# 204 low parts of weights from GpSimd to VectorE, with wider rotary tables and later gate rows

## The chip, the cores and the metric

The kernel runs on one core of a Trainium2 chip. The metric is the device time of one execution in microseconds. Three runs of the kernel before the change took 2226.13, 2218.59 and 2211.78 us; their median is 2218.59 us.

The engines are named as the profile names them: PE is the matrix engine (TensorE), DVE is VectorE, ACT is ScalarE, POOL is GpSimd, SP is SyncE, which here only issues DMA transfers.

## The reference

The kernel computes two layers of a hybrid decoder trunk on x of 1024 rows by 1024 columns, all in float32. The core of a layer:

```python
ada = c_act @ w_ada[l] + b_ada[l]
shift, scale, gate = jnp.split(ada, 3, axis=-1)
h = rmsnorm(x, norm_g[l]) * (1.0 + scale[:, None, :]) + shift[:, None, :]
p = h @ w_in[l]
mq, mk, mv, mo, mz, mi, mf, rq, rk, rv, rz = split_cols(p)
...
y_m = jax.nn.sigmoid(mo) * head_layernorm(cell, gn_m[l], N_HEADS_MLSTM) * jax.nn.silu(mz)
rq_h = rotary(rq.reshape(B, S, N_HEADS_RET, HD_R), positions)
rk_h = rotary(rk.reshape(B, S, N_HEADS_RET, HD_R), positions)
ret = retention_chunkwise(rq_h, rk_h, rv.reshape(B, S, N_HEADS_RET, HD_R))
y_r = head_layernorm(ret, gn_r[l], N_HEADS_RET) * jax.nn.silu(rz)
y = jnp.concatenate([y_m, y_r], axis=-1) @ w_out[l]
x = x + gate[:, None, :] * y
```

`rotary` multiplies halves of q and k by the cosine and the sine of position times a frequency per column. Four heads (0 to 3) are an mLSTM with a short causal convolution on q and k, four (4 to 7) are a retention. Each works in chunks and carries a state from chunk to chunk. A root mean square norm ends the trunk.

## The kernel before

Every matrix product is made of three: a float32 operand is split into a high part, which is the operand cast to the type that PE multiplies fast (float32r), and a low part, which is the operand minus its high part. `mm3` then multiplies high by high (L181), high by low (L182) and low by high (L183). For weights, `high` is a cast on ACT (L408, tile `wH`) and `low` is a subtraction of two 128 by 512 tiles (L413, tile `R`); its last argument names the engine, POOL unless said otherwise.

The work of a layer has three stages. In the **product stage** the columns of `w_in` are taken in jobs: a `plan` string gives their order (v for values of two heads, z, q, k and a for gates, queries, keys and output gates). A job multiplies a two by two block of weights by the hidden state with seven products instead of eight (named a11, a12, a22, S1 to S4), whose weights are sums of the blocks. A weight tile is loaded into `R`; for S1 and S3 a second block is added by a DMA that POOL issues (L714), for S2 and S4 the sum is made on DVE (L718). `Feeder.quad` states when, counted in slots (one slot is one product), a tile is loaded, cast and subtracted: the low part two slots ahead of its product. Products gather in four PSUM banks, two named px and two named pz, which DVE and ACT empty (L780 to L840). In front of the first job `build_forms` makes the sums of the hidden state (L639 to L660), whose high and low parts `split_to` makes on ACT and POOL (L881, L882).

**Attention** runs beside the later jobs of the product stage, one head after the other, by a table of steps. Its splits of q and k are L881 on ACT and L882 on POOL, that of the scores L1083 and L1084 (`sL`), that of the state L1107 and L1109 (`cL`); L934 makes the low part of the keys, L1185 a power on POOL that the norm's L1188 needs. For mLSTM heads the convolution is L894 on DVE. The **output projection** follows; its low parts are made on DVE for the first half of the columns and on POOL for the second.

Two side jobs run as generators beside the products; `yield n` lets n slots pass. `rotary_tables` (layer 0) makes the turns whose sines are taken later; all its DVE calls go through the wrapper in `Later`, so that the profile shows them at L148. `gate_rows` (layer 1, started by `adaptive`) loads sixteen rows of 256 KB through `ada_rows`, multiplies and sums them on DVE (L312, L314), adds a bias, splits the sum, spreads it over all partitions with PE (L350) and stores it. The output projection of layer 1 reads it back.

The order on PE is the order of the code. The orders on DVE, ACT, POOL and SP come from a scheduler that places instructions when the program is built; each engine then works through its list strictly in order. `late` keeps an instruction in the code's order.

Of the kernel before, what the change touches and what calls it, by code (L numbers as in the profile page):

```python
# [13 lines left out]
I32 = mybir.dt.int32  # L14
AF = mybir.ActivationFunctionType
ALU = mybir.AluOpType
# [3 lines left out]
P = 128  # L20

D = 1024
T = 1024
# [4 lines left out]
HALF = 512  # L28
CH = 256
# [8 lines left out]
NACC = 12  # L38
# [49 lines left out]
def tile_hybrid_trunk(ctx, tc, x, xt, c, positions, w_ada, b_ada, norm_g, w_in, w_blk, w_val, conv_w, conv_b,  # L88
                      b_igate, b_fgate, gn_m, gn_r, w_out, final_g, consts, out):
    nc = tc.nc  # L90
    V, A, G, PE, Q = nc.vector, nc.scalar, nc.gpsimd, nc.tensor, nc.sync
# [37 lines left out]
    turn = [0]  # L129
# [23 lines left out]
    def launch(gen, delay=0, last=0):  # L153
        uid[0] += 1
        pending.append([clock[0] + delay, uid[0] + last * 1000000, gen])
# [160 lines left out]
    def ada_columns_later(l):  # L316
        cl = cols[l][0]
        for half in range(2):
            k = 4 * half
            for which in range(2):  # L320
                accs = []
                yield from ada_rows(l, which * D + half * 512, accs)
                yield 1
                pt = ps_a()
                for i in range(4):
                    PE.matmul(pt[:, i:i + 1], accs[0][:, i * P:(i + 1) * P], ones, start=True, stop=True)
                yield 1
                if which:
                    t1 = wt("sm1", 4, 2)
                    V.scalar_tensor_tensor(t1, pt[:, 0:4], 1.0, cl[:, 112 + k:116 + k], ALU.add, ALU.add)  # L330
                    V.tensor_tensor(gsh[l][:, 0, k:k + 4], t1, cl[:, k:k + 4], ALU.mult)
                else:
                    V.tensor_tensor(gsh[l][:, 1, k:k + 4], pt[:, 0:4], cl[:, 104 + k:108 + k], ALU.add)

    def gate_rows(l):
        for half in range(2):
            accs = []
            yield from ada_rows(l, 2 * D + half * 512, accs)
            brow = wt("acc", 512, NACC)
            Q.dma_start(brow[0:1, :], b_ada[l, 2 * D + half * 512:2 * D + (half + 1) * 512].unsqueeze(0))  # L340
            yield 1
            acc = accs[0]
            V.tensor_tensor(acc[0:1, :], acc[0:1, :], brow[0:1, :], ALU.add)
            yield 1
            a2 = (wt("wH", 512, NW, F32R), wt("R", 512, NR, F32R))
            split_to(a2, acc)
            yield 2
            pt = ps_a()
            for i in range(2):
                PE.matmul(pt, ones_r, a2[i], start=i == 0, stop=i == 1)  # L350
            yield 1
            g = wt("acc", 512, NACC)
            V.tensor_copy(g, pt)
            yield 1
            Q.dma_start(gbd[half], g)

    def adaptive(l, gcol, gb):
        if l + 1 < DEPTH:
            yield from ada_columns_later(l + 1)
            yield from gate_cols(l, gcol)  # L360
        else:
            yield from gate_rows(l)

    def gate_cols(l, gcol):
        for half in range(2):
            accs = []
            yield from ada_rows(l, 2 * D + half * 512, accs)
            yield 2
            pt = ps_a()
            for i in range(4):  # L370
                PE.matmul(pt[:, i:i + 1], accs[0][:, i * P:(i + 1) * P], ones, start=True, stop=True)
            V.tensor_tensor(gcol[:, 4 * half:4 * half + 4], pt[:, 0:4],
                            cols[l][0][:, 120 + 4 * half:124 + 4 * half], ALU.add)
            yield 1
# [23 lines left out]
    def w_block(l, c0, p):  # L398
        return w_blk[l, (c0 - 8 * (c0 > OFF_I)) // P, p]
# [41 lines left out]

    rdr = [[dpool.tile([P, HALF], F32, name=f"rdr{i}{j}") for i in range(2)] for j in range(2)]

    def rotary_tables():
        V = Later()
        c1, c2, c3 = two_pi_split()
        ts = [wt("acc", 512, NACC) for _ in range(3)]
        ang, turn, tmp, rnd, a1, pos = (t[:, i * CH:(i + 1) * CH] for t in ts for i in range(2))
        a2 = ang
        for n in range(4):  # L450
            i, cs = n // 2, slice((n % 2) * CH, (n % 2 + 1) * CH)
            if n == 0:
                Q.dma_start(pos.bitcast(I32), positions[0:1, 0:CH].to_broadcast([P, CH]))
                yield 2
            V.tensor_copy(ang, pos.bitcast(I32))
            if n < 3:
                Q.dma_start(pos.bitcast(I32), positions[0:1, (n + 1) * CH:(n + 2) * CH].to_broadcast([P, CH]))
            V.tensor_scalar(ang, ang, kc[:, C_FREQ:C_FREQ + 1], None, ALU.mult)
            V.tensor_copy(a1.bitcast(F32R), ang)
            V.tensor_tensor(a2, ang, a1, ALU.subtract)  # L460
            V.tensor_scalar(turn, a1, c3, None, ALU.mult)
            V.scalar_tensor_tensor(turn, a2, c3, turn, ALU.mult, ALU.add)
            V.scalar_tensor_tensor(turn, a2, c2, turn, ALU.mult, ALU.add)
            yield 1
            for src, cc in ((a1, c2), (a2, c1), (a1, c1)):
                V.tensor_scalar(tmp, src, cc, None, ALU.mult)
                V.tensor_scalar(rnd, tmp, MAG_I, -MAG_I, ALU.add, ALU.add)
                V.tensor_tensor(tmp, tmp, rnd, ALU.subtract)
                V.tensor_tensor(turn, turn, tmp, ALU.add)
                yield 1  # L470
            parts = ((1, 0.0, tmp), (0, 0.25, a1))
            for which, sh, dst in parts:
                if sh:
                    V.tensor_scalar(turn, turn, sh, None, ALU.add)
                V.tensor_scalar(rnd, turn, MAG_I, -MAG_I, ALU.add, ALU.add)
                V.tensor_tensor(dst, turn, rnd, ALU.subtract)
                yield 1
                V.tensor_scalar(dst, dst, 0.49999994, -0.49999994, ALU.min, ALU.max)
            for which, sh, dst in parts:
                Q.dma_start(rdr[which][i][:, cs], dst)  # L480
            yield 1

    def gate_raw(l):
# [143 lines left out]
    def zcol(hg, m):  # L627
        return (OFF_MZ if hg < 4 else OFF_RZ) + (hg % 4) * HD + m * P

    def ocol(hg, m):  # L630
        return OFF_MO + hg * HD + m * P
# [29 lines left out]
            keep("U4", u4)  # L661
            yield 1

    POOL_LOW = ("S1", "S3", "a22")
    PRODUCT = {"a11": ("X", "11"), "S1": ("Z", "U1"), "S2": ("X", "U2"), "a12": ("Y", "21"), "S4": ("Z", "22"),
               "S3": ("X", "U3"), "a22": ("X", "U4")}
    VNAMES = ("a12", "a11", "S2", "S1", "S3", "a22", "S4")
# [13 lines left out]
    class Feeder:  # L681
# [21 lines left out]
        def quad(self, blk, at, u):  # L703
# [3 lines left out]
            def ev(t, fn, *args):  # L707
                self.events.append((t, lambda: fn(*args)))
# [22 lines left out]
            for n in at:  # L731
                if n not in ("S2", "S4"):
                    ev(at[n] - 4 + u, hi, n)
                    ev(at[n] - 2, lo, n, G if n in POOL_LOW else V)
            T2, T4 = at["S2"], at["S4"]
# [240 lines left out]
    def load_rotary(rot):  # L976
        for which in range(2):
            for i in range(2):
                t = wt("dm", 512, 2) if which == 0 else wt("nd", 516, 2) if i == 0 else bt()
                Q.dma_start(t[:, 0:HALF], rdr[which][i])  # L980
                A.activation(t[:, 0:HALF], t[:, 0:HALF], AF.Sin, scale=2.0 * math.pi)
                rot[which].append(t[:, 0:HALF])

    busy = [False]
# [490 lines left out]
    for l in range(DEPTH):  # L1475
# [4 lines left out]
        if l > 0:  # L1480
            cs = [w_block(l, col, p) for p in range(2) for col in (zcol(0, 0), ocol(0, 0), zcol(0, 1))]
# [17 lines left out]
        if l == 0:  # L1499
# [10 lines left out]
            for step in script.split():  # L1510
# [4 lines left out]
                if what in "SQ":  # L1515
                    half, tt, cc = arg
                    o, xi, acc = wt("acc", 512, NACC), xts[half][tt][cc], xss[half][:, tt, cc:cc + 1]
# [43 lines left out]
                elif what == "G":  # L1561
                    n = arg[0]
                    finish_gsh(0, 2 * n, 2, pad[:, 4 * n:4 * n + 2], pad[:, 4 * n + 2:4 * n + 4])
                elif what == "W":
                    i, p = arg
                    wsp[i, p] = high(rw[i][p], q3[:, p * 512:(p + 1) * 512] if i == 2 else None)
                else:
                    i, p = arg
# [19 lines left out]
        if l == 0:  # L1588
            for r in ring3:
                late(A.activation(r[:, :, HD:HD + 2], ident[:, 0:8].rearrange("p (a c) -> p a c", a=4), AF.Copy,  # L1590
                                  scale=0.0))
# [10 lines left out]
        gb = []  # L1602
        gcol = gsh[0][:, 0, :]
# [16 lines left out]

        slots = slot_order([what for what, _ in jobs])
        feed = Feeder(-1, [job_forms(j) for j in jobs], slots)
        launch(adaptive(l, gcol, gb), 2 if l else 30)

        def job_product(what, arg):
            h = arg[0]
# [33 lines left out]
        if l == DEPTH - 1:  # L1660
# [4 lines left out]
            for cc in range(2):  # L1665
                t = bt()
# [59 lines left out]
```

## Time and profile before

| | us |
|---|---|
| median of three runs | 2218.59 |
| the profiled execution | 2220.83 |
| its span, first to last instruction | 2219.1 |
| PE busy | 2116.1 |
| DVE busy | 1785.4 |
| ACT busy | 1141.9 |
| POOL busy | 949.2 |

The mean granted clock of PE was 0.985 of full speed. The profile is of one execution; its windows count from the span's start. A group row gives an instruction's line, engine, operation, its output and input tiles with shapes, how often it ran, its busy time and the mean time of one in ns, and the idle time of the engine in front of it with what ended that idle time. A row of the waits names the waiting engine and line, what it waited for, the time in all, how often, and the longest. A row of windows gives a stretch, then for each engine its busy time and number of instructions, the granted clock, the share of time that the DMA engines were busy, and GB/s. A row of the timeline gives the start, the duration, and the instruction.

### The profile page before, as it was taken

To read this page: it belongs to the slowest core of one execution; us is meant where nothing else is said; L and a number is where in the kernel's file an instruction comes from. 1 tells how busy PE (TensorE), PEld (TensorE's weight loads), DVE (VectorE), ACT (ScalarE), POOL (GpSimd) and SP (SyncE) were. 2 spreads that over 40 slices of the span, in tenths; PEclk is the share of its full clock that TensorE was granted. 3 is DMA by queue.
4 is the path that set the end of the run, shared out by engine and by line. 5 is a ranking of instruction groups with operands and counts; after the bars stand their busy time and mean duration, and the time that the engine had idled before them with its cause. 6 is when DMAs were issued, how large, how long until landed. Compare 5 with 4: busy or idle time off the path is not lost. (4 is left out here: it accounts for less than half of the span.)

```text
span 2219.1 us, 35050 instructions
## 1 busy us (share of the span) xinstructions
PE 2116.1 (95%) x11489; PEld 1827.4 (82%) x11489; DVE 1785.4 (80%) x3139; ACT 1141.9 (51%) x2151; POOL 949.2 (43%) x820
## 2 busy tenths in 40 slices
PE   7899999999999989999999999999999899999998
PEld 5698889888898878888887788888987887888887
DVE  6898888989989988874639697798897788988563
ACT  7535345445565656553544434444555556555342
POOL 1442345444453454424566344544444354442313
PEclk9999999999999999999999999999999999999999
DMA  8268678787796767686632867868866677687974
GB/s 291 58 189 216 189 218 252 218 241 210 211 249 179 203 188 205 190 270 231 214 105 69 246 198 200 229 184 224 228 189 183 177 214 194 166 211 244 231 251 120
DMA packets 452836, 448.44 MB, mean 202 GB/s; under 512 B 191314, under 2 KB 310042, under 8 KB 452652
## 3 DMA queue, kind: packets, MB, share of 16 engines
q1 hardware_dynamic: 432924, 410.27, 60.4%
q0 software_dynamic: 19584, 35.66, 10.6%
q8 instruction: 90, 1.47, 0.3%
q14 instruction: 94, 0.77, 0.1%
q10 hardware_dynamic: 144, 0.26, 0.0%
HBM read 322.76 MB, written 123.31 MB: 201 GB/s over the span
## 5 line engine op out<-in xcount | busy, mean ns | idle before, releaser
L408 ACT CAST wH<-R 128x512 fp32r<-128x512 f32 x616 | 377.6, 617 | 413.0 <-PE px L182 102.0
L413 POOL TENSOR_TENSOR R<-R,wH 128x512 fp32r<-128x512 f32 x276 | 393.9, 1437 | 457.3 <-ACT wH L408 290.0
L181 PE MATMUL px<-b,wH 128*128 128x512 f32 x912 | 361.1, 396 | 7.6 <-ACT acc L780 5.4
L182 PE MATMUL px<-b,wH 128*128 128x512 f32 x912 | 359.7, 394 | 0.0
L183 PE MATMUL px<-b,R 128*128 128x512 f32 x912 | 359.1, 394 | 0.0
L413 DVE TENSOR_TENSOR R<-R,wH 128x512 fp32r<-128x512 f32 x340 | 263.5, 778 | 98.7 <-ACT wH L408 93.4
L182 PE MATMUL pz<-b,wH 128*128 128x512 f32 x704 | 275.5, 391 | 1.6 <-DVE b L1271 1.6
L181 PE MATMUL pz<-b,wH 128*128 128x512 f32 x704 | 276.0, 392 | 0.0
L183 PE MATMUL pz<-b,R 128*128 128x512 f32 x704 | 275.1, 391 | 0.0
L181 PEld LDWEIGHTS px<-b,wH 128*128 128x128 f32 x912 | 173.5, 190 | 43.9 <-ACT acc L780 6.9
L183 PEld LDWEIGHTS px<-b,R 128*128 128x128 f32 x912 | 173.6, 190 | 37.5
L181 PE MATMUL px<-wH,b 128*128 128x256 f32 (+1 forms) x576 | 176.4, 306 | 26.8 <-DVE acc L837 12.6
L182 PEld LDWEIGHTS px<-b,wH 128*128 128x128 f32 x912 | 173.6, 190 | 33.2
L182 PE MATMUL px<-R,b 128*128 128x256 f32 (+1 forms) x576 | 175.5, 305 | 8.3 <-DVE R L413 8.3
L183 PE MATMUL px<-wH,b 128*128 128x256 f32 (+1 forms) x576 | 174.7, 303 | 0.0
L714 POOL DMA_DIRECT2D R<-in_w_blk_dram x104 | 92.8, 892 | 186.3 <-DMA R<-in_w_blk_dram 85.0
L183 PEld LDWEIGHTS pz<-b,R 128*128 128x128 f32 x704 | 132.6, 188 | 28.4
L182 PEld LDWEIGHTS pz<-b,wH 128*128 128x128 f32 x704 | 132.5, 188 | 27.5 <-DVE b L1271 2.3
L181 PEld LDWEIGHTS pz<-b,wH 128*128 128x128 f32 x704 | 132.7, 188 | 25.7 <-issue 0.2
L181 PEld LDWEIGHTS px<-wH,b 128*128 128x128 f32 x576 | 115.5, 201 | 31.5 <-issue 13.1
L181 PE MATMUL pz<-wH,b 128*128 128x256 f32 (+1 forms) x448 | 134.7, 301 | 1.3 <-DVE acc L790 1.2
L882 POOL TENSOR_TENSOR kc<-acc,kc 128x512 fp32r<-128x512 f32 x64 | 87.4, 1366 | 109.7 <-ACT kc L881 91.6
(343 smaller groups left out, 5327.0 us busy)
## 6 DMA issues: line engine op xcount, KB each, us to landing
R<-in_w_blk_dram SPq DMA_DIRECT2D x276, 256.0 KB
vdr<-acc SPq DMA_DIRECT2D x128, 256.0 KB
ring<-vdr SPq DMA_DIRECT2D x64, 512.0 KB
R<-in_w_out_dram SPq DMA_DIRECT2D x128, 256.0 KB
R<-in_w_blk_dram POOLq DMA_DIRECT2D x104, 256.0 KB, 4.5
R<-in_w_val_dram SPq DMA_DIRECT2D x80, 256.0 KB
gdr<-acc SPq DMA_DIRECT2D x64, 256.0 KB
acc<-in_w_ada_dram SPq DMA_DIRECT2D x64, 256.0 KB
```

The lines of the kernel that those rows point to most:

```text
L181: PE.matmul(o, lt[0], rt[0], start=start, stop=False, skip_group_check=more)
L182: PE.matmul(o, lt[0], rt[1], start=False, stop=False, skip_group_check=more)
L183: PE.matmul(o, lt[1], rt[0], start=False, stop=stop, skip_group_check=more)
L408: A.copy(h, r)
L413: eng.tensor_tensor(lo, r, f(h), ALU.subtract)
L714: G.dma_start(raw[n], src, accum_op=ALU.add)
L882: eng.tensor_tensor(dst[1], src, f(dst[0]), ALU.subtract)
```

## The change

Three things change. The tuple of products whose low part is made on POOL becomes empty, so that `Feeder.quad` gives all of them to DVE. That moves 204 of the 278 low parts that POOL makes, 102 in each layer's product stage; those of `load_w`, of layer 1's first three blocks and of the output projections do not depend on it and stay on POOL. The rotary tables are made in two pieces of 512 columns instead of four of 256, with three more tiles of the large pool, without the limiting to just under a half; a slightly smaller scale of the sine (6.283185) stands for that. In layer 1 `gate_rows` starts 40 slots after the first product instead of 2.

```diff
+    SIN_SCALE = 6.283185
+
     def rotary_tables():
...
-        ts = [wt("acc", 512, NACC) for _ in range(3)]
-        ang, turn, tmp, rnd, a1, pos = (t[:, i * CH:(i + 1) * CH] for t in ts for i in range(2))
+        ang, tmp, a1 = (wt("acc", 512, NACC) for _ in range(3))
+        turn, rnd, pos = (bt() for _ in range(3))
...
-        for n in range(4):
...
+        for i in range(2):
             V.tensor_copy(ang, pos.bitcast(I32))
-            if n < 3:
...
+            if i == 0:
...
-                V.tensor_scalar(dst, dst, 0.49999994, -0.49999994, ALU.min, ALU.max)
...
-                Q.dma_start(rdr[which][i][:, cs], dst)
+                Q.dma_start(rdr[which][i], dst)
...
-    POOL_LOW = ("S1", "S3", "a22")
+    POOL_LOW = ()
...
-                A.activation(t[:, 0:HALF], t[:, 0:HALF], AF.Sin, scale=2.0 * math.pi)
+                A.activation(t[:, 0:HALF], t[:, 0:HALF], AF.Sin, scale=SIN_SCALE)
...
-        launch(adaptive(l, gcol, gb), 2 if l else 30)
+        launch(adaptive(l, gcol, gb), 40 if l else 30)
```

On POOL, at the first products of layer 0, the list before reads (b is a tile of the hidden state's sums, R a low part or a weight being added to):

```order
L882 TENSOR_TENSOR b_1262<-acc_1247,b_1261 128x512
L413 TENSOR_TENSOR R_1491<-R_1312,wH_1489 128x512
L413 TENSOR_TENSOR R_1495<-R_1318,wH_1493 128x512
L413 TENSOR_TENSOR R_1588<-R_1325,wH_1586 128x512
L882 TENSOR_TENSOR b_1439<-acc_1435,b_1438 128x512
L413 TENSOR_TENSOR R_1592<-R_1333,wH_1590 128x512
L413 TENSOR_TENSOR R_1663<-R_1541,wH_1661 128x512
L882 TENSOR_TENSOR b_1485<-acc_1481,b_1484 128x512
```

and after the change, from the same place:

```order
L882 TENSOR_TENSOR b_1262<-acc_1247,b_1261 128x512
L882 TENSOR_TENSOR b_1439<-acc_1435,b_1438 128x512
L882 TENSOR_TENSOR b_1488<-acc_1484,b_1487 128x512
L882 TENSOR_TENSOR b_1532<-acc_1528,b_1531 128x512
L882 TENSOR_TENSOR b_1574<-acc_1570,b_1573 128x512
L714 DMA R_1808<-in_w_val_dram 128x512
```

The splits of the sums now follow each other on POOL, and the adding DMAs come directly behind them.

On DVE, a little later, the last rows in front of the first L837, which empties a px bank, are before:

```order
L148 TENSOR_SCALAR acc_1445<-acc_1446 128x256
L148 SCALAR_TENSOR_TENSOR acc_1444<-acc_1444 128x256
L148 TENSOR_SCALAR acc_1445<-acc_1445 128x256
L148 SCALAR_TENSOR_TENSOR acc_1444<-acc_1444 128x256
L148 TENSOR_TENSOR acc_1445<-acc_1445 128x256
L148 TENSOR_TENSOR acc_1444<-acc_1444,acc_1445 128x256
L148 TENSOR_SCALAR acc_1445<-acc_1444 128x256
L413 TENSOR_TENSOR R_1745<-R_1304,wH_1743 128x512
L148 TENSOR_SCALAR acc_1445<-acc_1445 128x256
L148 TENSOR_TENSOR acc_1445<-acc_1445 128x256
L837 TENSOR_TENSOR acc_1619<-px_1402,acc_1619 128x512
```

and after:

```order
L413 TENSOR_TENSOR R_1656<-R_1538,wH_1654 128x512
L639 TENSOR_TENSOR acc_1570<-b_970,b_971 128x512
L660 SCALAR_TENSOR_TENSOR acc_1570<-acc_1568,acc_1570 128x512
L148 TENSOR_SCALAR acc_1444<-acc_1444,kc 128x512
L413 TENSOR_TENSOR R_1660<-R_1540,wH_1658 128x512
L413 TENSOR_TENSOR R_1736<-R_1304,wH_1734 128x512
L148 CAST acc_1446<-acc_1444 128x512
L148 TENSOR_TENSOR acc_1444<-acc_1444,acc_1446 128x512
L148 TENSOR_SCALAR b_1447<-acc_1446 128x512
L837 TENSOR_TENSOR acc_1615<-px_1402,acc_1615 128x512
```

Fourteen rotary rows (L148) stand ahead of L837 before and five after; five low parts that were POOL's stand between the first L831 and it, and a sixth just ahead of that L831.

At the same place of layer 1, DVE's rows in front of L837 are before:

```order
L639 TENSOR_TENSOR acc_13886<-b_12961,b_12962 128x512
L660 SCALAR_TENSOR_TENSOR acc_13886<-acc_13884,acc_13886 128x512
L314 SCALAR_TENSOR_TENSOR acc_13711<-acc_13807,cact,acc_13711 128x512
L314 SCALAR_TENSOR_TENSOR acc_13711<-acc_13894,cact,acc_13711 128x512
L413 TENSOR_TENSOR R_14050<-R_13623,wH_14048 128x512
L837 TENSOR_TENSOR acc_13931<-px_13724,acc_13931 128x512
```

and after:

```order
L413 TENSOR_TENSOR R_13836<-R_13593,wH_13834 128x512
L660 SCALAR_TENSOR_TENSOR acc_13781<-acc_13779,acc_13781 128x512
L413 TENSOR_TENSOR R_13901<-R_13789,wH_13899 128x512
L660 SCALAR_TENSOR_TENSOR acc_13821<-acc_13819,acc_13821 128x512
L413 TENSOR_TENSOR R_13905<-R_13791,wH_13903 128x512
L413 TENSOR_TENSOR R_13976<-R_13564,wH_13974 128x512
L837 TENSOR_TENSOR acc_13863<-px_13662,acc_13863 128x512
```

The two L314 of the gate rows are gone from here (they stand among the retention heads' rows L964 to L966 now), and low parts have come in.

More of the change, by code (lines that the diff above doesn't have):

```diff
@@ L446, in rotary_tables @@
         c1, c2, c3 = two_pi_split()
-        ts = [wt("acc", 512, NACC) for _ in range(3)]
-        ang, turn, tmp, rnd, a1, pos = (t[:, i * CH:(i + 1) * CH] for t in ts for i in range(2))
+        ang, tmp, a1 = (wt("acc", 512, NACC) for _ in range(3))
+        turn, rnd, pos = (bt() for _ in range(3))
         a2 = ang
-        for n in range(4):
[L451 to L454, printed above, removed]
+        Q.dma_start(pos.bitcast(I32), positions[0:1, 0:HALF].to_broadcast([P, HALF]))
+        yield 2
+        for i in range(2):
             V.tensor_copy(ang, pos.bitcast(I32))
-            if n < 3:
-                Q.dma_start(pos.bitcast(I32), positions[0:1, (n + 1) * CH:(n + 2) * CH].to_broadcast([P, CH]))
+            if i == 0:
+                Q.dma_start(pos.bitcast(I32), positions[0:1, HALF:T].to_broadcast([P, HALF]))
+            yield 1
             V.tensor_scalar(ang, ang, kc[:, C_FREQ:C_FREQ + 1], None, ALU.mult)
@@ L460, in rotary_tables @@
             V.tensor_tensor(a2, ang, a1, ALU.subtract)
+            yield 1
             V.tensor_scalar(turn, a1, c3, None, ALU.mult)
@@ L467, in rotary_tables @@
                 V.tensor_scalar(rnd, tmp, MAG_I, -MAG_I, ALU.add, ALU.add)
+                yield 1
                 V.tensor_tensor(tmp, tmp, rnd, ALU.subtract)
@@ L470, in rotary_tables @@
                 yield 1
-            parts = ((1, 0.0, tmp), (0, 0.25, a1))
-            for which, sh, dst in parts:
+            for which, sh, dst in ((1, 0.0, tmp), (0, 0.25, a1)):
                 if sh:
@@ L476, in rotary_tables @@
                 V.tensor_tensor(dst, turn, rnd, ALU.subtract)
-                yield 1
-                V.tensor_scalar(dst, dst, 0.49999994, -0.49999994, ALU.min, ALU.max)
-            for which, sh, dst in parts:
-                Q.dma_start(rdr[which][i][:, cs], dst)
+                yield 2
+                Q.dma_start(rdr[which][i], dst)
             yield 1
```

## The prediction

> **What bounds the kernel now.** I read the page's busy times first, then a table by stage, then what TensorE (PE) waits for, and last single instructions of VectorE (DVE) and GpSimd (POOL).
>
> ```profile
> span 2219.1 us, 35050 instructions
> PE 2116.1 (95%) x11489; PEld 1827.4 (82%) x11489; DVE 1785.4 (80%) x3139; ACT 1141.9 (51%) x2151; POOL 949.2 (43%) x820
> ```
>
> PE is busy 95% of the span, so all that any change off PE can win is PE's idle time and the slower clock that goes with it. The stages show where that is. The cuts are mine: product stage of layer 0 without and with attention, output projection, and the same for layer 1.
>
> ```profile
> core 0: us, PE busy (x) PEld busy (x) DVE busy (x) ACT busy (x) POOL busy (x), PEclk, DMA share, GB/s
> 105.00:350.00 245.00, 228.94 (x1378) 206.25 (x1379) 215.07 (x385) 103.66 (x183) 88.32 (x72) 0.96 0.71 202
> 350.00:945.00 595.00, 576.82 (x3208) 502.42 (x3207) 531.69 (x978) 334.45 (x660) 280.65 (x257) 0.99 0.77 213
> 945.00:1195.00 250.00, 245.43 (x1137) 200.25 (x1135) 153.50 (x223) 122.90 (x200) 115.14 (x87) 1.00 0.58 187
> 1195.00:1400.00 205.00, 192.34 (x1166) 172.18 (x1167) 168.10 (x264) 86.44 (x160) 93.25 (x67) 0.98 0.72 201
> 1400.00:2030.00 630.00, 606.86 (x3385) 530.88 (x3384) 531.39 (x976) 347.59 (x684) 288.20 (x267) 0.98 0.72 198
> ```
>
> In the four product stages PE is idle 16.1, 18.2, 12.7 and 23.1 us: 70 us together. The clock column costs 0.04 x 245 + 0.01 x 595 + 0.02 x 205 + 0.02 x 630 = 32 us more, so that a microsecond of idling carries about 0.45 us of slow clock with it (32/70). DVE is the next engine: 89% busy in the attention stage of layer 0, 84% in that of layer 1. PE's waits, longest first, name it:
>
> ```profile
> PE px L181 <- DVE acc L837: 12.6, 3, 5.3
> PE pa L1126 <- POOL sL L1084: 10.8, 8, 3.4
> PE px L182 <- DVE R L413: 8.3, 3, 5.6
> PE px L181 <- DVE acc L894: 5.7, 2, 4.9
> PE pa L183 <- DVE b L934: 4.3, 6, 1.0
> PE pa L1135 <- DVE cL L1109: 3.8, 3, 1.7
> ```
>
> No row of that list is a low part of GpSimd (POOL R L413): those are ready in time today. PE waits for DVE's attention and bank-emptying work, and for one POOL result, sL.
>
> **The low parts.** The order shows 204 of POOL's 278 low parts moved (276 of them are in the profile), 102 in each layer; the other 74, the output projections' among them, stay. One costs 1.44 us on POOL and 0.60 us on DVE, from start to start of neighbours (1236.69 to 1237.29 below):
>
> ```profile
> L413 POOL TENSOR_TENSOR R<-R,wH 128x512 fp32r<-128x512 f32 x276 | 393.9, 1437 | 457.3 <-ACT wH L408 290.0 <-issue 65.7 <-DMA b<-xdr 26.6
> ...
> L413 DVE TENSOR_TENSOR R<-R,wH 128x512 fp32r<-128x512 f32 x340 | 263.5, 778 | 98.7 <-ACT wH L408 93.4
> ...
> 1234.17 1.99 DVE L314 SCALAR_TENSOR_TENSOR acc<-acc,cact,acc 128x512 f32<-128x512 f32 x1 [1.10 <-DMA acc<-in_w_ada_dram]
> 1236.09 0.68 DVE L805 SCALAR_TENSOR_TENSOR acc<-px,acc 128x512 fp32r<-128x512 f32 x1
> 1236.69 0.68 DVE L413 TENSOR_TENSOR R<-R,wH 128x512 fp32r<-128x512 f32 x1
> 1237.29 0.68 DVE L840 TENSOR_TENSOR acc<-pz,acc 128x512 f32<-128x512 f32 x1
> ...
> 1239.68 0.74 DVE L314 SCALAR_TENSOR_TENSOR acc<-acc,cact,acc 128x512 f32<-128x512 f32 x1
> ...
> 1234.01 1.59 POOL L413 TENSOR_TENSOR R<-R,wH 128x512 fp32r<-128x512 f32 x1
> ```
>
> So DVE gains 204 x 0.60 = 122 us of work and POOL loses 204 x 1.44 = 293. But these rows show a second effect: the same DVE instruction L314 takes 0.74 us alone and 1.99 us when a POOL low part started just before it. Two forms of one line show which instructions suffer:
>
> ```profile
> L894 DVE SCALAR_TENSOR_TENSOR acc<-acc,cols,acc x96: 712/744/1874, 529.2 to 1928.0; 128x512 f32<-128x512 f32 x96
> L894 DVE SCALAR_TENSOR_TENSOR acc<-pz,cols,acc x48: 700/742/753, 525.5 to 1907.9; 128x511 f32<-128x511 f32 x16, 128x510 f32<-128x510 f32 x16, 128x509 f32<-128x509 f32 x16
> ```
>
> (shortest/median/longest ns.) With both large operands in SBUF an instruction stretches to 1874 ns; with one in PSUM (pz) it never passes 753. The Trainium skill's page "SBUF — State Buffer", in its section on the two separate sides, says that GpSimd and a VectorE instruction with two SBUF inputs lock each other out for a whole instruction. By that rule a low part could hold VectorE for all of its duration, and the trace agrees in kind.
>
> This delay is refunded when the low part leaves POOL. Its size per low part is not a row, so it is bounded. From above: L314 at its longest here, 1.99 - 0.74 = 1.25 us. From below: the DVE low parts alone stretch by 340 x (0.778 - 0.684, the usual 0.68) = 32 us, over all of POOL's 820 instructions 0.04 us each. Going through the DVE instructions one by one and putting each stretched one to the POOL instruction that it overlaps most, 142 belong to the 204 low parts, 132 us in all, 0.65 us per low part; the first and the last of them:
>
> ```profile
> 114.50 2.60 DVE L639 TENSOR_TENSOR acc<-b,b 128x512 f32<-128x512 f32 x2
> ...
> 2020.53 1.39 DVE L859 SCALAR_TENSOR_TENSOR acc<-acc,acc 128x512 f32<-128x512 f32 x1 [0.85 <-ACT acc L857]
> ```
>
> I take 0.65. Net for DVE: 122 - 132 = -10 us; with the bounds, -133 to +114. That is the main point: DVE's load hardly changes, and POOL's falls by a third.
>
> What that is worth on PE, by place. **Layer starts** (105 to 350 and 1195 to 1400): L837 empties the bank that PE waits for. By the order (its rows stand in the section on the change) five or six low parts are added in front of it; at 0.60 against 0.65 they cancel. But nine of the fourteen rotary instructions ahead of it in layer 0 go, and the five left are longer: 14 x 0.4 less 5 x 0.5, by the rows of the next part, is 3 us. In layer 1 one L312 and two L314 of the gate rows leave, 0.5 and twice 0.74 to 1.99, also some 3 us. So L837 comes about 3 us earlier in each layer: 6 of the 12.6 us of that wait, with the clock (x 1.45) **-9 us**. It cannot be more than -15, and if the stretching stays (POOL's own L882 takes the freed turns) it is +3. **Attention stages**: sL stands in POOL's queue behind fewer low parts, and of its 10.8 us I let 3 go: -4 us with the clock (bounds 0 and -16). What hides the low parts themselves is that they are early: no wait of PE for POOL's shows. On DVE, though, each stands in line and holds those behind it while its high part (ACT, L408) is late; there it is the attention's L1062, L1104, L1109 and the emptying L790, and PE waits for them. DVE's own low parts show the size. In each pair of rows the first are L413's instructions in the stage, the second DVE's waits there:
>
> ```profile
> core 0: us, DVE busy (x) POOL busy (x), PEclk, DMA share, GB/s
> 350.00:945.00 595.00, 73.14 (x93) 100.71 (x69) 0.99 0.77 213
> ...
> DVE R L413 <- ACT wH L408: 7.9, 7, 2.9
> ...
> 1400.00:2030.00 630.00, 78.28 (x98) 103.41 (x74) 0.98 0.72 198
> ...
> DVE R L413 <- ACT wH L408: 22.5, 14, 4.5
> ```
>
> That is 30.4 us for 191 low parts, 0.16 us each; 143 more (69 + 74) bring 23 us, less 143 x 0.05 of refund over cost, +16 us on a DVE that has 63 and 99 us of room in these stages. A tenth of it on PE is +2, so the attention stages come to **-2 us** (bounds -16 and +24, all of it with the clock).
>
> **Rotary tables.** 104 instructions of 256 columns become 48 of 512, and the 8 clamps go.
>
> ```profile
> L148 DVE TENSOR_SCALAR acc<-acc 128x256 f32<-128x256 f32 x48 | 17.9, 385 | 0.6
> L148 DVE TENSOR_TENSOR acc<-acc,acc 128x256 f32<-128x256 f32 x24 | 13.2, 552 | 0.5
> L148 DVE TENSOR_TENSOR acc<-acc 128x256 f32<-128x256 f32 x12 | 6.1, 507 | 0.2
> L148 DVE SCALAR_TENSOR_TENSOR acc<-acc 128x256 f32<-128x256 f32 x8 | 5.4, 676 | 0.0
> ...
> L312 DVE TENSOR_SCALAR acc<-acc,cact 128x512 f32<-128x512 f32 x8 | 4.9, 607 | 0.0
> ```
>
> These four rows are 42.6 us of DVE. After: 22 two-tensor ones at 0.60 and 26 one-tensor ones at 0.40 to 0.61 (L312), 24 to 29 us. DVE gets some 15 us back in its 245 us stage, where it is 88% busy (215/245). Beyond the 3 in front of L837, already counted, that is **-2 us** on PE, bounds 0 and -6. Six of its twelve transfers go from SP's queue, too small to matter. The sine's new scale changes no instruction's cost.
>
> **Gate rows of layer 1.** Sixteen 256 KB loads and two stores on SP, 16 DVE instructions, two high and two low parts and four PE matmuls move from the layer's first products to some 40 slots later, into the beginning of attention. They cost the same there, but DVE is fuller and 'acc' buffers are wanted by attention: **+2 us**, bounds -3 and +10. Their result is needed only after the products.
>
> Sum: -9 - 2 - 2 + 2 = -11 us. The profiled execution took 2220.8 us, 2.2 over the median of 2218.6 and inside the runs' scatter (2211.8 to 2226.1): 2220.8 - 11 = **2210 us**.
>
> **The rivals.** *DVE becomes the bound (slower).* If POOL's other instructions (L882, L1084) meet DVE as often as the low parts did, the refund falls to about 0.3 us. For: DVE has more two-input instructions to meet. Against: there is less on POOL to meet. In the attention stages that is 143 x 0.30 = 43 us more, and 66 with the waits for high parts. In six of the 24 stretches of 50 us there, the first and the last of them here, DVE has no gaps already:
>
> ```profile
> 400.00:450.00 50.00, 49.53 (x260) 42.45 (x259) 49.22 (x90) 18.82 (x37) 19.92 (x16) 1.00 0.71 199
> ...
> 1900.00:1950.00 50.00, 48.30 (x247) 41.02 (x246) 49.74 (x90) 31.72 (x61) 20.76 (x21) 1.00 0.69 191
> ```
>
> There all of it reaches PE, and where the backlog spills over some more: a third of 66, 22 x 1.45 = +32: **2253 us**. It decides once the refund is under about 0.45 us. The Trainium skill's "Perfetto Trace Analysis", section on optimizing Scalar/DVE operations, advises to take work off a saturated VectorE, even to GpSimd, which speaks against this change, and adds that between these two it might not help. Without any refund a third of 143 x 0.60 + 23 would reach PE, 36 x 1.45 = +53 us.
>
> *The whole POOL queue counts (faster).* If two thirds of PE's waits for L837, sL, L894, L934 and L1109 go (37.2 us), 25 x 1.45 = -36: **2185 us**. For: DVE itself waits for POOL's short L1185, and a shorter POOL queue serves it sooner. Against: transfers, which the change does not touch, stand in the same chain of waits.
>
> ```profile
> DVE nmu L1188 <- POOL rsd L1185: 23.5, 20, 4.2
> ...
> 1665.66 4.34 DMA acc<-qdr
> ```
>
>
> *Hidden anyway.* Low parts are early today and stay so; only noise is left: **2219 us**.
>
> **Chances.** Forecast 0.36 (own range 2197 to 2221), hidden 0.14, faster 0.28, slower 0.22. One per cent, 22 us, is what a measurement here can tell from no change. Faster by more: the faster rival and a bit of the forecast, 0.30; slower by more: 0.20; between: 0.50. The range 2175 to 2254 takes in both rivals' middles.
>
> **What would show it.** POOL busy near 650 us, DVE near 1765 (over 1850 means no refund); L314 and L894 (acc form) closer to their medians; the wait for L837 down from 12.6 to about 5. PE waiting for DVE R L413 in attention, or DVE at 98% through whole attention stages, would prove me wrong.

## The result, and the profile after

The changed kernel takes 2188.75 us (median; 2185.83 to 2191.57), against 2222.36 us (2211.78 to 2231.77) for the kernel before on the same chip. The ratio is 0.9864, 95% interval [0.9836, 0.9891]: 1.4% faster, some 30 us by the ratio. The forecast was 2210 us, the range 2175 to 2254. The profiled execution of the changed kernel, from its page:

```profile
span 2188.9 us, 34934 instructions
PE 2105.7 (96%) x11489; PEld 1818.2 (83%) x11489; DVE 1775.1 (81%) x3287; ACT 1149.3 (53%) x2151; POOL 671.1 (31%) x616
```

DVE does 204 low parts more (and 56 rotary instructions fewer) and is busy for 10 us less (1785.4 before); POOL loses 278 us. For the same 11489 products PE is idle 83.2 us where it was 103.0, and busy for 10.4 us less, at a granted clock of 0.989 where it was 0.985. The table by stage, with the same stretches as in the prediction:

```profile
105.00:350.00 245.00, 239.81 (x1522) 218.47 (x1523) 211.59 (x385) 112.76 (x198) 50.92 (x43) 0.99 0.77 219
350.00:945.00 595.00, 575.67 (x3142) 498.06 (x3142) 532.65 (x1050) 337.82 (x659) 180.89 (x183) 0.99 0.77 214
945.00:1195.00 250.00, 244.50 (x1163) 200.76 (x1162) 155.16 (x213) 123.32 (x202) 121.93 (x91) 1.00 0.53 173
1195.00:1400.00 205.00, 200.34 (x1188) 177.52 (x1187) 165.86 (x291) 87.95 (x162) 47.81 (x41) 0.99 0.77 214
1400.00:2030.00 630.00, 610.39 (x3408) 534.23 (x3407) 551.52 (x1086) 358.09 (x694) 187.33 (x188) 0.99 0.75 207
```

PE is idle 5.2 us in the first start (16.1 before) and 4.7 in the second (12.7), and the clock there went from 0.96 to 0.99 and from 0.98 to 0.99. To say where the time went, I compared the start of the same matrix product in both profiles at each boundary. The five stretches give 17.0, -2.4, 0, 8.8 and 7.0 us, 30 together: most of it in the two layer starts. A run whose program is the same as before's in layer 0 differs there by up to 5 us for a stretch, so a stretch is known to about that.

What PE still waits for at the places that the prediction spoke of:

```profile
PE pa L1126 <- ACT sH L1083: 8.2, 4, 4.1
PE pa L1126 <- POOL sL L1084: 6.3, 7, 2.9
PE pa L183 <- DVE b L934: 5.4, 6, 1.7
PE px L181 <- DVE acc L894: 5.0, 1, 5.0
PE px L181 <- DVE acc L837: 3.5, 2, 2.1
```

L837 fell from 12.6 to 3.5, and the wait for cL (L1109, 3.8 before) is gone from the list. The row of sL fell from 10.8 to 6.3, but the same products (L1126) now wait longer for sH, the high part of the scores, which ACT makes. Before, that row was

```profile
PE pa L1126 <- ACT sH L1083: 4.7, 5, 1.4
```

Together L1126 waits 14.5 us where it waited 15.5, so that PE wins only about 1 us there. Of the low parts and of the instructions that they stretched:

```profile
L413 DVE TENSOR_TENSOR R<-R,wH 128x512 fp32r<-128x512 f32 x544 | 404.2, 748 | 123.4 <-ACT wH L408 121.1 <-POOL b L1324 1.5
L413 POOL TENSOR_TENSOR R<-R,wH 128x512 fp32r<-128x512 f32 x72 | 96.6, 1344 | 164.8 <-ACT wH L408 145.8 <-issue 9.9 <-DMA b<-xdr 4.8
L314 DVE SCALAR_TENSOR_TENSOR acc<-acc,cact,acc 128x512 f32<-128x512 f32 x56 | 45.4, 811 | 4.1 <-DMA acc<-in_w_ada_dram 4.0
L894 DVE SCALAR_TENSOR_TENSOR acc<-acc,cols,acc 128x512 f32<-128x512 f32 x96 | 78.9, 823 | 0.0
```

L314 took 1040 ns in the mean before and takes 811 now, the form of L894 with both large operands in SBUF 954 and now 823. Going through DVE's instructions one by one, as the prediction did, all stretching together falls from 277 to 164 us. That is 113 us, 0.55 us for each moved low part (up to 0.6, by what is taken as the unstretched time of a row). DVE's wait for high parts grew from 93.4 to 121.1 us.

### The profile page after: what moved, and what is told of

Read it like the earlier page. It is cut to its first block, busy times and chain, and to the rows that moved or that the text cites. A ratio compares the mean times of both kernels' runs of the same rounds, so it can differ in the third digit from the quotient of the medians.

```text
span 2188.9 us, 34934 instructions
## 1 busy us (share of the span) xinstructions
PE 2105.7 (96%) x11489; PEld 1818.2 (83%) x11489; DVE 1775.1 (81%) x3287; ACT 1149.3 (53%) x2151; POOL 671.1 (31%) x616
## 4 chain that ended last, share of the span: by engine, by line
PE 47%; DVE 11%; DMA 5%; issue 3%; ACT 1%; POOL 1%; SPq 1%; DVEq 0%; POOLq 0%; ACTq 0%
PE px L181 6%; PE px L182 6%; PE px L183 6%; PE pz L181 5%; PE pz L182 5%; PE pz L183 4%; PE pa L183 4%; PE pa L181 3%; PE pa L182 3%; DVE R L413 2%; DVE acc L894 2%; PE pa L1135 1%; DMA acc<-kfr 1%; PE pa L1045 1%; DVE R L718 1%
## 5 line engine op out<-in xcount | busy, mean ns | idle before, releaser
L413 DVE TENSOR_TENSOR R<-R,wH 128x512 fp32r<-128x512 f32 x544 | 404.2, 748 | 123.4 <-ACT wH L408 121.1
L181 PE MATMUL px<-wH,b 128*128 128x256 f32 (+1 forms) x576 | 173.2, 301 | 13.8 <-DVE acc L894 5.0
L183 PE MATMUL px<-wH,b 128*128 128x256 f32 (+1 forms) x576 | 171.9, 298 | 0.0
L882 POOL TENSOR_TENSOR kc<-acc,kc 128x512 fp32r<-128x512 f32 x64 | 91.7, 1434 | 193.3 <-ACT kc L881 169.3
L413 POOL TENSOR_TENSOR R<-R,wH 128x512 fp32r<-128x512 f32 x72 | 96.6, 1344 | 164.8 <-ACT wH L408 145.8
L882 POOL TENSOR_TENSOR q<-acc,q 128x512 fp32r<-128x512 f32 x64 | 93.5, 1461 | 131.8 <-ACT q L881 123.5
```

The lines of the kernel that those rows point to most:

```text
L181: PE.matmul(o, lt[0], rt[0], start=start, stop=False, skip_group_check=more)
L183: PE.matmul(o, lt[1], rt[0], start=False, stop=stop, skip_group_check=more)
L413: eng.tensor_tensor(lo, r, f(h), ALU.subtract)
L882: eng.tensor_tensor(dst[1], src, f(dst[0]), ALU.subtract)
```

## The experiments

**Theory at the start:** what pays is that DVE is no longer held up by POOL's low parts, and this outweighs what DVE takes over. **Rivals:** the shorter queue of POOL pays (the "faster" rival of the prediction), or the rotary tables and gate rows do. First each part alone, and all but one.

### The low parts alone

```diff
-    POOL_LOW = ("S1", "S3", "a22")
+    POOL_LOW = ()
```

> The kernel before with the 204 low parts on VectorE, rotary tables and gate rows as before. Theory A (the gain is the refund of the port delay): most of the change's -34 us, so 2188 to 2200, VectorE's busy time within 15 us of before. Theory B (rotary tables and gate rows are the gain, the low parts cancel): 2215 to 2225.

Measured: 2200.19 us, ratio 0.9918 [0.989, 0.9946], about 18 us of the 30. PE's wait for L837 is 4.7 us. DVE is busy 1783.9 us, against 1785.4 before: 204 low parts more cost it nothing.

### The rotary tables alone, the gate rows alone, both

```diff
-    POOL_LOW = ()
+    POOL_LOW = ("S1", "S3", "a22")
...
-        launch(adaptive(l, gcol, gb), 40 if l else 30)
+        launch(adaptive(l, gcol, gb), 2 if l else 30)
```

With both edits, the changed kernel keeps only its new rotary tables; with the first alone it keeps tables and gate rows; the kernel before, with the start at slot 40, has the gate rows alone.

> The kernel before with the wide rotary tables alone. Theory A: -3 us for 15 us of VectorE work in layer 0's start, so 2215 to 2222. Theory B: -10 us or more, 2205 to 2213, all of it before 350 us.

> The kernel before with the gate rows of layer 1 started 40 slots in. Theory A: -5 us near 1220 to 1370, given back as attention starts, 2215 to 2225. Theory B: a lasting gain of 8 us or more, 2205 to 2214.

> The changed kernel with the 204 low parts back on GpSimd, so rotary tables and gate rows alone are changed. Theory A: at most -8 us, 2212 to 2222. Theory B: 2188 to 2200, as the full change.

Measured: rotary tables 0.998 [0.9964, 0.9997], gate rows 1.0033 [1.0013, 1.0052], both 1.0019 [1.0002, 1.0036]. The wait for L837 hardly moves: 10.5, 12.7 and, with both,

```profile
PE px L181 <- DVE acc L837: 12.5, 3, 5.3
```

So the prediction's reason for L837 to come earlier (fewer rotary rows and gate rows ahead of it) does not hold. What does it is seen in the timelines ahead of L837 in layer 0. First with both edits but the low parts on POOL, then the whole change:

```profile
119.53 2.39 DVE L639 TENSOR_TENSOR acc<-b,b 128x512 f32<-128x512 f32 x2
120.00 3.06 POOL L413 TENSOR_TENSOR R<-R,wH 128x512 fp32r<-128x512 f32 x2 [0.95 <-ACT wH L408]
121.84 2.38 DVE L660 SCALAR_TENSOR_TENSOR acc<-acc,acc 128x512 f32<-128x512 f32 x2
```

```profile
119.35 1.28 DVE L639 TENSOR_TENSOR acc<-b,b 128x512 f32<-128x512 f32 x2
120.56 0.68 DVE L660 SCALAR_TENSOR_TENSOR acc<-acc,acc 128x512 f32<-128x512 f32 x1
121.16 0.68 DVE L413 TENSOR_TENSOR R<-R,wH 128x512 fp32r<-128x512 f32 x1
121.76 0.68 DVE L660 SCALAR_TENSOR_TENSOR acc<-acc,acc 128x512 f32<-128x512 f32 x1
```

Two L639 and two L660 take 4.7 us beside two low parts of POOL. In the changed kernel the same four and one low part take 3.1 us.

### The change without one part

The change with gate rows at slot 2 (low parts and rotary tables), and low parts with the later gate rows but the old tables:

```diff
-        launch(adaptive(l, gcol, gb), 40 if l else 30)
+        launch(adaptive(l, gcol, gb), 2 if l else 30)
```

> The changed kernel with the gate rows started at slot 2 as before: low parts and rotary tables alone. The runs so far give the gate rows +4 to +7 us of cost with the low parts on GpSimd. If that holds beside the moved low parts, 2180 to 2186; if the later start is what frees layer 1's start, 2193 to 2200.

> The changed kernel with the rotary tables as before: low parts and gate rows alone. If the parts add up, low parts -19 and gate rows +7: 2205 to 2212. If the gate rows help once VectorE is free at layer 1's start, 2190 to 2200.

Measured: 2187.03 us, 0.9847 [0.9833, 0.9862], and 2207.86 us, 0.9948 [0.9927, 0.9968]. The first is as good as the whole change and, by its ratio, the best kernel here. The later gate rows come out 0.2 to 0.4% slower in all four pairs, 4 to 9 us, though in the pairs with the low parts each difference lies within its uncertainty. Low parts and tables together bring more than their sum: 0.9918 times 0.998 would be 0.990.

### The same low parts made twice

Behind each moved low part POOL makes it again into the same tile. That is redundant work.

```diff
                 r[n] = low(h[n], raw[n], eng)
+                if n in ("S1", "S3", "a22"):
+                    G.tensor_tensor(r[n], raw[n], f(h[n]), ALU.subtract)
```

> The changed kernel in which GpSimd makes each of the 204 low parts once more behind VectorE's, into the same tile, so that GpSimd has its old load and VectorE keeps its new one. Theory A (what the change wins is VectorE's freedom from GpSimd's low parts): VectorE's instructions stretch by some 130 us again on top of the 122 us added, and the time is at or above before, 2215 to 2245. Rival (low parts were won because VectorE makes them sooner, or the gain is the rotary tables): GpSimd's second making takes little, 2188 to 2205.

Measured: 2268.09 us, 1.0208 [1.0183, 1.0233]. The page, and the second makings among POOL's groups (L726 by this kernel's lines):

```profile
PE 2132.0 (94%) x11489; PEld 1835.2 (81%) x11489; DVE 1890.6 (83%) x3287; ACT 1147.1 (51%) x2151; POOL 965.3 (43%) x820
...
L726 POOL TENSOR_TENSOR R<-R,wH 128x512 fp32r<-128x512 f32 x204 | 299.0, 1468 | 406.1 <-DVE R L413 286.4 <-issue 38.2 <-DVE va L1184 15.6
```

DVE runs the very instructions of the changed kernel and needs 115 us more for them (1890.6 against 1775.1). My count gives 115 us to the second makings, 0.56 us each: the refund, measured from the other side. The Trainium skill's page "SBUF — State Buffer" says in its section on the two separate sides that GpSimd and a VectorE instruction with two SBUF inputs lock each other out for a whole instruction; the run agrees in kind, and the size for this kernel is the 0.56 us. The 76 us against the change (1.0208 less 0.9864) are not the stretching alone: the second making also stands in POOL's queue, and the product has to wait for it (PE waits 6.7 us for L726, once).

### Half of the low parts

Only the low parts of the first 56 slots of each layer on DVE, or only the later ones:

```diff
-                    ev(at[n] - 2, lo, n, G if n in POOL_LOW else V)
+                    ev(at[n] - 2, lo, n, G if n in POOL_LOW and at[n] < EARLY else V)
```

(this is the run with the later ones; the other has the comparison the other way round, as >= EARLY, with EARLY = 56 and the old tuple in both).

> The changed kernel with only the low parts of the first 56 slots of each layer on VectorE (46 of 204). If the layer starts hold the gain (28 of 30.6 us by the place of the same PE instruction in both traces), 2188 to 2198. If attention's share is as large, 2203 to 2215.

> All three edits, but only the low parts of the later slots (from the 56th of each layer on) go to VectorE; those of the first 56 slots stay on GpSimd. It is the other half of the run with the early ones alone. If the two halves add up, the late ones are worth the rest, about 20 us against the run without any: 2200 to 2206 us, ratio 0.990 to 0.994, and the wait for L837 stays near 12. If the prediction's sum were right (-2 us for the attention stages), the late ones would be worth nothing: 2218 to 2226.

Measured: early ones 2212.12 us, 0.996 [0.9944, 0.9975]; later ones 2210.9 us, 0.9964 [0.9945, 0.9983]. Against the run without any (1.0019) each half is worth 12 to 13 us, both 34. The 9 us beyond the sum are as large as the uncertainty of the four ratios. So the low parts of the layer starts, not quite a quarter of all, bring as much as all the others, but those bring their 12 us too: by the start of the same products the run with the later ones wins 12 us in the two attention stretches on the run without any. The wait for L837 follows the early ones; its row with the early ones on DVE, and with the later ones (one line further down in both kernels):

```profile
PE px L181 <- DVE acc L838: 3.5, 2, 2.1
```

```profile
PE px L181 <- DVE acc L838: 10.5, 2, 5.3
```

### Why the tables pay only with the low parts

In the run with the low parts alone, DVE stands still at a rotary row until a tile of the round before is stored (from the timeline), and PE then for a bank that ACT empties late (from the waits of 180 to 245 us):

```profile
204.25 0.29 DVE L148 CAST acc<-acc 128x256 fp32r<-128x256 f32 x1 [5.45 <-DMA rdr<-acc]
```

```profile
PE px L181 <- ACT acc L780: 5.5, 1, 5.5
```

DVE waits for such stores three times there, 10.2 us in all. Before, it was once and 2.0 us: a slower DVE came later to that row. To test it, the two results of each round go to tiles of their own:

```diff
-        a2 = ang
+        a2 = ang; sto = (bt(), bt())
...
-            parts = ((1, 0.0, tmp), (0, 0.25, a1))
+            parts = ((1, 0.0, sto[0][:, cs]), (0, 0.25, sto[1][:, cs]))
```

> The low parts alone on VectorE, with the rotary tables of before (256 columns, clamps and all), except that their two results are written to buffers of their own, so that no rotary instruction has to wait until a tile of the round before is stored. Theory (the part of the gain that only the low parts and the new tables together bring comes from that wait: VectorE stood 5.5 us at a rotary instruction in the run with the low parts alone): the wait is gone, and the time is 2188 to 2194 us, ratio 0.985 to 0.989. Rival (the fewer rotary instructions bring it): 2198 to 2204 us, as with the low parts alone.

Measured: 2189.61 us, 0.9862 [0.9827, 0.9897], as fast as the change, with the narrow tables and their clamps. No L148 waits for a store, and between 180 and 245 us no wait of PE is left in the list. The stage 105 to 350, of the low parts alone and with the stores apart:

```profile
105.00:350.00 245.00, 233.68 (x1431) 210.44 (x1432) 212.15 (x428) 104.03 (x184) 44.78 (x39) 0.97 0.72 208
```

```profile
105.00:350.00 245.00, 238.70 (x1515) 216.88 (x1516) 216.26 (x438) 111.46 (x197) 49.14 (x42) 0.99 0.76 217
```

By the start of the same products, the low parts alone win 6.3 us on before in this stretch and the run with the stores apart 16.2: 9.9 of the 10.6 us between the two medians (by the ratios 0.56%, known to 0.45%). So it was the wait for stores that made the new tables worth more, not their fewer instructions. That these stores cost little while the low parts are on POOL rests on the 2.0 us alone; tiles of their own without the moved low parts were not run.

### POOL kept busy without the stretching

Behind each moved low part POOL does idle work on a dead tile of 8 columns: a select that reads the high part, so that POOL waits for it as it did for a low part, and nine fills.

```diff
                 r[n] = low(h[n], raw[n], eng)
+                if n in ("S1", "S3", "a22"):
+                    G.affine_select(cth, f(h[n])[:, 0:KT], [[1, KT]], ALU.is_ge, 0.0, base=0, channel_multiplier=1)
+                    for _ in range(9):
+                        G.memset(cth, 1.0)
```

> All three edits, and behind each of the 204 moved low parts GpSimd runs ten tiny instructions of its own (one select that reads 8 columns of the same high part, then nine fills of 8 columns, by the rows of such fills about 0.1 us each, some 1.2 us together). This is work that the reference doesn't need, into a tile that nobody reads any more. VectorE's order stays as in after, but for one swap. So GpSimd's queue is about as long, and waits for the same high parts, as before the change, but it reads and writes next to nothing. Theory (VectorE is freed because the two engines no longer hold each other up at SBUF): the time stays near the change's, 2186 to 2195 us, ratio 0.985 to 0.990, and VectorE's busy time near 1775. Rival (GpSimd's shorter queue brings the gain: sL and L1185 come earlier): most of the gain is gone, 2205 us or more, with VectorE's busy time still near 1775 and PE's waits for sL back at 8 to 11 us.

Measured: 2202.55 us, 0.9934 [0.9911, 0.9958]: between the two expectations. PE waits 10.6 us for L934 (5.4 in the change) and 11.1 us for sL, counting the 3.2 put down to the idle work ahead of it (6.3 in the change). The groups of POOL:

```profile
L724 POOL MEMSET cth<- 128x8 f32 x1836 | 202.3, 110 | 99.2
...
L724 POOL TENSOR_SCALAR_AFFINE_SELECT cth<-wH 128x8 f32<-128x8 f32 x204 | 92.3, 452 | 327.2 <-ACT wH L408 324.3
```

With the gaps between the fills (99 us) a piece occupies POOL for 1.9 us, where a low part took 1.44. So two further runs: six fills instead of nine, and nine fills without the select.

> As the run that kept GpSimd busy, but with six fills instead of nine, so that each piece of idle work takes about 1.4 us, as long as a low part did (1.44), where the run before had 1.9. If GpSimd's queue costs by its length, the loss of 14 us against the change shrinks by more than a quarter: 2195 to 2200 us. If what costs is that each piece stands in GpSimd's queue until its high part is there, however short it is, the loss stays: 2200 to 2204 us.

> The same with nine fills and without the select, so that GpSimd is as busy (about 1.4 us for each moved low part) but waits for no high part. If the wait for the high part at the head of GpSimd's queue is what delays sL, L1185 and the splits of q and k, the time is back at the change's: 2187 to 2193 us. If the length of the queue alone does it: 2195 to 2202 us.

Measured: with six fills 2194.22 us, 0.9894 [0.9873, 0.9915]. The loss against the change goes with the length of the queue: 0.7% at 1.9 us, 0.3% at 1.4, each known to 0.35% and their difference to 0.32%, where the wait for the high part is the same. The run without the select (2215.61 us, 0.9984) decides nothing: fills that wait for nothing were placed at the program's beginning, where they hold up other work (ACT's L380 waits 16.2 us behind them),

```profile
PE pa L387 <- ACT b L380: 14.6, 2, 14.2
```

and 14 of its 27 us are lost before the first products. In all three the stretching stays at 164 to 172 us by my count. So the six-fill run gives the shares: without the stretching, but with POOL's queue about as long as before (875.9 us busy and 67 us of gaps between the fills, against 942.1), the kernel is 1.25% faster than with neither (0.9894 against 1.0019), 28 us; the shorter queue brings another 0.3%, 7 us, no more than its uncertainty.

### The other splits too, and the low parts later

From the change with gate rows at slot 2. First all splits of L882 (q, k and the first forms) on DVE; then the moved low parts one slot later in the order.

```diff
-    def split_to(dst, src, eng=G):
+    def split_to(dst, src, eng=V):
```

```diff
-                    ev(at[n] - 2, lo, n, G if n in POOL_LOW else V)
+                    ev(at[n] - 2 + (n in ("S1", "S3", "a22")), lo, n, V)
```

> Low parts and rotary tables, gate rows at the start as before, and the 164 other low parts that GpSimd makes in one piece (L882: those of q and k in attention and of the first forms) go to VectorE too, each right behind its high part. If the exchange of work against stretching holds for these as well, VectorE's busy time stays within 15 us of 1770 and the time is 2180 to 2192 us. If the waits for the high parts count (the splits stand directly behind their high parts, unlike the moved ones), VectorE waits some 50 us more at L882, and the time is 2195 to 2215 us.

> Low parts and rotary tables, gate rows at the start as before, and the moved low parts put one slot later into VectorE's order, one slot before the products that read them. VectorE then waits less for their high parts (121 us in the run this one starts from). If these waits cost time on TensorE, as the prediction had it (+23 us of waits, +2 us on TensorE), it becomes faster by 2 to 8 us: 2179 to 2185. If TensorE is now kept waiting for low parts, its waits for R L413 rise from 8 us, and the time is above 2190.

Measured: all splits 2198.66 us, 0.9911 [0.9883, 0.994], 0.6% slower than the kernel it starts from. The stretching falls to 53 us and DVE's busy time to 1763.8, so the exchange of work holds here too. But DVE now stands in front of these splits, and PE behind it (DVE's and PE's waits; the last was 5.5 us):

```profile
DVE kc L882 <- ACT kc L881: 48.3, 26, 5.6
DVE q L882 <- ACT q L881: 18.7, 13, 3.5
...
PE pa L183 <- DVE b L934: 16.8, 7, 6.7
```

Low parts later: 2204.01 us, 0.9932 [0.9915, 0.9949], 0.85% slower than the kernel it starts from, some 19 us (17 between the medians). Neither theory holds: DVE waits for the high parts nearly as long (121.5 us there), and PE waits no longer for a low part (7.9 us, 8.3 in the change):

```profile
DVE R L413 <- ACT wH L408: 118.5, 79, 16.5
```

By the start of the same products it loses 9.7 us in the attention of layer 0 and 6.3 in that of layer 1. Which step of the new order costs this stays open. It may be that a weight's buffers come free a slot later, which wasn't tried.

## Why the prediction was right or wrong

**What bounds the kernel: right.** The time came from PE's idle time and the clock beside it. In the first layer start a microsecond of idling carried more clock than the 0.45 taken: idle fell by 10.9 us and 0.03 of clock on 245 us is 7.4 more. Over the whole program 19.8 us of idling and 10.4 us of clock went, 0.53 to one.

**Low parts against refund: right.** Taken were 0.60 of cost against 0.65 of refund. The refund was 0.55 by count and 0.56 by putting it back, and DVE's busy time moved by -1.5 (low parts alone) and +2.0 us (1773.1 to 1775.1 with the other edits): they cancel. The rival "DVE becomes the bound" needed less than 0.45. The price that the prediction gave without any refund, +53 us, is close to the +2.1%, 46 us, of the run that put the stretching back, in part by chance, since that run also has the new tables' gain and PE's wait for the second making in it. The Trainium skill's page "Perfetto Trace Analysis", section on optimizing Scalar/DVE operations, says that taking work off a saturated VectorE, even to GpSimd, may make sense, and adds that between these two it might not help. Here the move the other way won 18 us, the gain of the low parts alone.

**Layer starts: this step failed.** The prediction let the low parts cancel in front of L837, gave its 3 us to the rotary and gate rows, and put an end at -15 us, for which it shows no sum (all 12.6 us of L837 with the clock would be 18). Measured: tables and gate rows without the low parts leave L837 at 12.5 and the kernel 0.2%, 4 us, slower than before; the early low parts, moved beside them, take L837 to 3.5. So the -9 us stood with the wrong edits: what was to bring nothing at this place, the low parts, brought the gain. That they cancel over the whole program says nothing of the rows in front of one instruction: there POOL's low parts stretched just the sums that the first banks wait for. And the end at -15 was no end: the two stretches won 26 us against before and 21 against the run that has all but the low parts, since other waits of PE went with it (in the first start L780 2.0, L326 1.9 and L964 1.4 us, in the second L830 from 2.9 to 0.5), and the clock rose.

**Attention stages (-2) and gate rows (+2): mis-sized.** With the gate rows, the change wins 5 us in the two stretches against before, and 13 against the run that has all but the low parts (2.8 in layer 0, 10.5 in layer 1); the bounds were -16 and +24. The run with the later low parts says the same, 12 us. So this term was too small by some 10 us, and the path that it named is only a part: the row of sL gave 4.5 us where 3 were taken, but 3.5 of them came back as the wait for sH. Which other waits carry the rest isn't isolated; the 3.8 us for cL are one that went. DVE's wait for high parts in these stages, 30.4 us in the prediction's two rows, is now (350 to 945, then 1400 to 2030)

```profile
DVE R L413 <- ACT wH L408: 14.5, 15, 2.3
DVE R L413 <- ACT wH L408: 32.3, 27, 5.4
```

46.8 us: 16 more, where 23 were predicted. None of the runs shows that it costs PE anything: the run that was to shorten that wait didn't. The gate rows cost 4 to 9 us.

**Rotary tables (-2): right alone, wrong together.** Alone they bring 4 us (1 to 8). With the low parts it is 16 to 19 (0.9847 against 0.9918, 0.9864 against 0.9948), because a faster DVE runs into stores that were hidden by its being late. The prediction saw the six fewer transfers and called them too small to matter; what counted was which row waits for them.

**The rival that gave the time.** 2185 us was that of POOL's queue. That it came close to the time is luck: kept at the same length, the queue takes back only some 7 us, and of the five waits of which it let 25 us go, 17 went (L837 9.1, sL 4.5, cL 3.8, L894 0.7, while L934 rose by 1.1). DVE's wait for L1185 fell from 23.5 to 14.5 us.

**What was to be seen:** POOL near 650 (671), DVE near 1765 (1775), L837 near 5 (3.5), L314 and L894 nearer to their medians: all seen, L837 for another reason. The signs that would have spoken against it did not come: PE's wait for DVE's low parts is 8.3 us as before, and DVE is 88 to 90% busy in the attention stages.

## What to carry to other kernels

Where two engines hold each other up at a memory, count the stretched instructions: work that moves to the fuller engine may cost it nothing, and the gain comes where the stretched rows stand in front of a wait, not where the averages are. Moved work must not stand directly behind a late producer: low parts placed two slots ahead paid, splits behind their own high part did not. When an engine gets faster, look for waits that its lateness hid, stores of reused tiles above all; a tile more cured one of them here.

## What was not expected of the hardware

Small selects and fills on POOL hardly stretch DVE: 1836 fills and 204 selects of 8 columns left DVE's stretching at 172 us by count, with 0.5 us put to the selects, while 204 subtractions of 128 by 512 brought 115 us. So it is not POOL's being busy that slows DVE (946.3 us busy in that run, 949.2 before), but what it does. The fills read nothing and the selects only 8 columns; which of the two spares DVE, the small size or the missing reads, the runs don't separate. And the same 204 instructions one slot later in DVE's order cost some 19 us, at nearly the same busy time of DVE (1777.3 against 1769.4) and nearly the same waits for high parts (118.5 against 121.5): the order is worth about as much as moving the low parts alone was, and why stays open.
